# Rotary embedding over split heads: the cosine and sine tables loaded in pieces of 120 and 8 partitions

## The chip, the cores and the metric

The kernel runs on one core of one Trainium2 chip. The core has a matrix engine (PE, TensorE), a vector engine (DVE), a scalar engine (ACT), a general engine (POOL, GpSimd), a queue engine (SP, SyncE) and sixteen DMA engines, which all transfers share. The metric is the device time of one execution in microseconds; a comparison takes the median of several executions. The profiles come from one further execution each, taken by the hardware profiler; "span" is the time from its first to its last instruction.

## The reference

The input x has 16 batches, 512 positions and 1024 columns in float32; the columns are 16 heads of 64. Each head is split in two halves of 32, and the halves are rotated by tables that depend on the position alone:

```
x = x.reshape(batch, seq, num_heads, head_dim)
x1, x2 = x[..., :half_dim], x[..., half_dim:]
cos = cos[None, :, None, :]      # tables are (512, 32)
sin = sin[None, :, None, :]
rotated = concatenate([x1 * cos - x2 * sin, x1 * sin + x2 * cos], axis=-1)
```

33.6 MB go in and 33.6 MB come out; each table has 64 KB.

## The kernel before

All memory is laid out by hand, and each engine has its own list of instructions; the order of work is set by these lists and by semaphores, not by a scheduler.

**Tiles.** The work is ten tiles. Batches 0, 1, 14 and 15 are tiles of their own ("singles"): 128 partitions, 4 positions of 1024 numbers in each (2 MB). The other twelve batches go in six pairs: 128 partitions, 8 positions in each (4 MB). A position row of a tile, 128 x 1024, is one unit of compute; there are 64 units. x lies in a ring of 40 rows, in which the result replaces the input, so the first six tiles find free room and the last four wait for a store to free theirs.

**Compute.** For a unit, DVE multiplies x by cosine into PSUM (L293), POOL multiplies x with its halves swapped by the signed sine into SBUF (L257; six units are done by DVE at L286), and the sum is made in one of two ways: DVE adds (L304), or PE adds the sine product onto the PSUM tile by a matmul with the identity (L224) and ACT copies the sum back (L191).

**Tables.** Cosine and sine are each loaded once into `stage`, as 128 partitions of 4 positions x 32 numbers (L174, 512 bytes in each partition). For singles DVE copies cosine into PSUM (L264), and ACT writes sine with its two signs to SBUF (L182, L183). Pairs hold two batches over 128 partitions, and so need each position in two partitions: PE makes that from `stage` with a picking matrix (L208), ACT writes the signed sine of it (L186, L187). The picking matrix is made by ACT (L177) from an identity that POOL builds (L235, L237).

**Queues.** All loads are issued by ACT (L153 and L174), all stores by SP (L161). ACT's list begins with load 0, then cosine, then sine, then loads 1 to 5, and only then its compute; the last four loads stand between its later additions, each after a wait for the store that frees its room. A transfer adds 16 to its semaphore. Those who use the tables wait for 16 on `sem_cos` (DVE ahead of L264, PE ahead of L208) and on `sem_sin` (ACT ahead of L182, PE ahead of L208). POOL's first product waits for ACT's L183, and SP's first store for the last sum of tile 0.

Of the kernel before, what the change touches and what calls it, by code (L numbers as in the profile page):

```python
# [6 lines left out]
def bass_split_heads_rope_kernel(  # L7
# [20 lines left out]
    P = 128  # L28
    R1 = seq // P
# [34 lines left out]
    EH = H * HD // BANK  # L64
    LEAD = 1
    LAG = 10

    with ExitStack() as stack:
        x_sb = stack.enter_context(nc.sbuf_tensor([P, RING, H, 2, HALF], fp32))
        t2_sb = stack.enter_context(nc.sbuf_tensor([P, NT2, H, 2, HALF], fp32))  # L70
        stage = stack.enter_context(nc.sbuf_tensor([P, 2, R1 * HALF], fp32))
# [11 lines left out]
        sem_cos = stack.enter_context(nc.semaphore("cos"))  # L83
        sem_sin = stack.enter_context(nc.semaphore("sin"))
# [16 lines left out]
        def c_of(t, r):  # L101
            return c1_ps[:, r, :] if tiles[t][1] == R1 else pair_ps[:, r // R1, 0, r % R1, :]
# [19 lines left out]
        def where(u):  # L122
            t, r = rows[u]
            return t, r, u % RING

        def swapped(k):
            return x_sb[:, k, :, ::-1, :]

        def over_heads(table):
            return table[:, None, :, :].broadcast_to([P, H, 2, HALF])  # L130
# [8 lines left out]
        def wait_t2_free(eng, u):  # L139

            if u >= NT2:
                v = u - NT2
                if PE2[v]:
                    eng.wait_ge(sem_e, n_pe[v])
                else:
                    eng.wait_ge(sem_v, n_comb[v])

        def stores_of(k):

            return sum(b * R1 // R2 == k for b, _ in tiles)  # L150

        def load(eng, t):
            eng.dma_start(in_sbuf(t), in_dram(x1, x2, t)).then_inc(sem_in[t], 16)  # L153
# [10 lines left out]
        def on_scalar(ae):  # L164
            later = {}
            for t, (b, n) in enumerate(tiles):
                if b * R1 + n <= RING:
                    load(ae, t)
                else:

                    later.setdefault((b * R1 - RING) // R2 * R2 + R2 - 1 + LAG, []).append(t)
                if t == 0:
                    for i, (table, sem) in enumerate(((cos, sem_cos), (sin, sem_sin))):
                        ae.dma_start(stage[:, i, :], table.rearrange("(s r) d -> s (r d)", r=R1)).then_inc(sem, 16)  # L174

            ae.wait_ge(sem_i, 2)
            ae.activation(  # L177
                pick[:], ident[:].rearrange("q (s k) -> q k s", k=2)[:, :, :, None].broadcast_to([P, 2, P // 2, 2]), COPY
            ).then_inc(sem_g, 1)
            ae.wait_ge(sem_sin, 16)  # L180
            sv = stage[:, 1, :].rearrange("s (r d) -> s r d", d=HALF)
            ae.activation(s1_sb[:, :, 0, :], sv, COPY, scale=-1.0)  # L182
            ae.activation(s1_sb[:, :, 1, :], sv, COPY).then_inc(sem_s, 1)  # L183
            ae.wait_ge(sem_t, 2)
            s2 = s2_sb[:].rearrange("p (k r) t d -> p k r t d", r=R1)
            ae.activation(s2[:, :, :, 0, :], pair_ps[:, :, 1, :, :], COPY, scale=-1.0)  # L186
            ae.activation(s2[:, :, :, 1, :], pair_ps[:, :, 1, :, :], COPY).then_inc(sem_s, 1)  # L187
            for u in range(NU):
                if PE2[u]:
                    ae.wait_ge(sem_e, n_pe[u])  # L190
                    ae.activation(xs[:, u % RING, :], t1_ps[:, u % NT1, :], COPY).then_inc(sem_a, 1)  # L191
                for t in later.get(u, ()):
                    k = (tiles[t][0] * R1 - RING) // R2
                    ae.wait_ge(sem_out[k], 16 * stores_of(k))
                    load(ae, t)

        def on_tensor(pe):
            pe.wait_ge(sem_z, 1)
            for k in range(NT1):
                for b in range(EH):  # L200
                    pe.matmul(  # L201
                        t1_ps[:, k, b * BANK:(b + 1) * BANK], zero[:, 0:P], zero[:], start=True, stop=True
                    ).then_inc(sem_w, 1)
            pe.wait_ge(sem_g, 1)
            pe.wait_ge(sem_cos, 16)
            pe.wait_ge(sem_sin, 16)
            for k in range(2):
                pe.matmul(  # L208
                    pair_ps[:, k].rearrange("p c r d -> p (c r d)"),
                    pick[:, k].rearrange("q s b -> q (s b)"),  # L210
                    stage[:].rearrange("q c f -> q (c f)"),
                    start=True,
                    stop=True,
                ).then_inc(sem_t, 1)
            for u in range(NU):
                if not PE2[u]:
                    continue
                pe.wait_ge(sem_m, u + 1)

                if not V2[u]:  # L220
                    pe.wait_ge(sem_p, n_pool[u])
                t2 = t2_sb[:, u % NT2, :, :, :].rearrange("p h t d -> p (h t d)")
                for b in range(EH):
                    ins = pe.matmul(  # L224
                        t1_ps[:, u % NT1, b * BANK:(b + 1) * BANK],
                        ident[:],
                        t2[:, b * BANK:(b + 1) * BANK],
                        start=False,
                        stop=True,
                        skip_group_check=True,  # L230
                    )
                ins.then_inc(sem_e, 1)
# [27 lines left out]

        def on_vector(ve):
            ve.memset(zero[:], 0.0).then_inc(sem_z, 1)  # L262
            ve.wait_ge(sem_cos, 16)
            ve.tensor_copy(c1_ps, stage[:, 0, :].rearrange("s (r d) -> s r d", d=HALF)).then_inc(sem_c, 1)  # L264
            ve.wait_ge(sem_c, 1)
            ve.wait_ge(sem_w, NT1 * EH)

            def pair_tables():
                ve.wait_ge(sem_s, 2)
                row = pair_ps[:, V_ROW // R1, 1, V_ROW % R1, :]  # L270
                ve.tensor_scalar_mul(v_ps[:, 0, :], row, -1.0).then_inc(sem_c, 1)
                ve.tensor_copy(v_ps[:, 1, :], row).then_inc(sem_c, 1)

            first_v = V2.index(True)

            def mul(u):
                t, r, k = where(u)
                if r == 0:
                    ve.wait_ge(sem_in[t], 16)
                if (t, r) == (2, 0):  # L280
                    pair_tables()
                if u == first_v:
                    ve.wait_ge(sem_c, 3)
                if V2[u]:
                    wait_t2_free(ve, u)
                    ve.tensor_tensor(t2_sb[:, u % NT2, :, :, :], swapped(k), over_heads(v_ps), mult)  # L286
                if u >= NT1:
                    v = u - NT1
                    if PE2[v]:
                        ve.wait_ge(sem_a, n_pe[v])  # L290
                    else:
                        ve.wait_ge(sem_v, n_comb[v])
                ve.tensor_tensor(  # L293
                    t1_ps[:, u % NT1, :].rearrange("p (h d) -> p h d", d=HALF),
                    x_sb[:, k, :, :, :].rearrange("p h t d -> p (h t) d"),
                    c_of(t, r)[:, None, :].broadcast_to([P, 2 * H, HALF]),
                    mult,
                ).then_inc(sem_m, 1)

            def comb(u):  # L300
                t, r, k = where(u)
                ve.wait_ge(sem_m, u + 1)
                ve.wait_ge(sem_p, n_pool[u])  # L303
                ve.tensor_tensor(  # L304
                    xs[:, k, :],
                    t1_ps[:, u % NT1, :],
                    t2_sb[:, u % NT2, :, :, :].rearrange("p h t d -> p (h t d)"),
                    add,
                ).then_inc(sem_v, 1)

            for u in range(NU + LEAD):
                if u < NU:
                    mul(u)
                if u >= LEAD and not PE2[u - LEAD]:
                    comb(u - LEAD)

        on_sync(nc.sync)
        on_scalar(nc.scalar)
        on_gpsimd(nc.gpsimd)
        on_tensor(nc.tensor)  # L320
        on_vector(nc.vector)


# [31 lines left out]
```

## Time and profile before

| what | value |
|---|---|
| time, median of 3 runs | 161.21 us (161.02 to 161.35) |
| span of the profiled execution | 160.3 us |
| moved by DMA | 67.26 MB, 419 GB/s over the span |
| HBM read and written | 33.69 MB and 33.55 MB |
| DVE, POOL busy | 130.3 us, 134.9 us |
| PE, ACT busy | 72.8 us, 24.4 us |
| loads of x, 4 MB: issue to landing | 38.0 us (median of 6) |
| stores, 4 MB: issue to landing | 25.0 us (median of 6) |
| cosine, sine: issue to landing | 7.8 us, 7.5 us |

In lines of the profile, times are in microseconds. In the page's slices each digit is a share of 1/40 of the span, in tenths. A group's line names the source line, the engine, the operation and its tiles. In the timeline the first number is the start, the second the duration, and brackets tell how long the engine stood idle before and what ended that. In the table of stretches a row begins with the stretch and its length, then come the busy times of PE, PE's weight load, DVE, ACT and POOL, the clock granted to PE, the share of time in which the DMA engines were busy, and GB/s. A waits line gives the sum, the number of waits and the longest. "ACTq" and "SPq" are the queues' issuing of transfers.

The trace also records each packet of the DMA engines with its start, duration and size (not the engine it ran on), and each increment that a transfer makes on its semaphore when it lands.

### The profile page before, as it was taken

The numbers are of one execution on the slowest core, as the hardware profiler recorded it, in microseconds if no ns is written. First come the engines' busy times: TensorE is split into PE (matmuls) and PEld (weight loads), VectorE is DVE, ScalarE is ACT, GpSimd is POOL, SyncE is SP. The second block draws the span as 40 slices with busy tenths as digits, with TensorE's granted clock in tenths as the row PEclk, the third lists the DMA queues.
The fourth block names the chain that finished last, engine by engine and source line by source line (L and its number), as shares of the span: only waits on it lengthen the run. The fifth ranks groups of instructions, "written<-read, shape, count | busy, mean of one in ns | idle before, by whom it ended". The sixth has DMA issues, their size and how long they took to land.

```text
span 160.3 us, 522 instructions
## 1 busy us (share of the span) xinstructions
PE 72.8 (45%) x94; PEld 24.0 (15%) x94; DVE 130.3 (81%) x117; ACT 24.4 (15%) x27; POOL 134.9 (84%) x64
## 2 busy tenths in 40 slices
PE   6050004478357936660847105489458435850000
PEld 1020002022202211210221002022202111220000
DVE  0069998599989999996999709899889999999500
ACT  0420000203120222022012010201220402040000
POOL 1059999999999999999999999699999999289400
PEclk9955555557755587689687965555555977699555
DMA  5999999999999999999999999999999999999896
GB/s 147 409 441 474 409 450 409 425 429 429 446 429 458 417 411 466 409 433 401 450 433 425 425 409 458 409 433 433 411 429 462 441 417 401 450 441 441 376 450 294
DMA packets 3170, 67.26 MB, mean 419 GB/s; under 512 B 352, under 2 KB 608, under 8 KB 608
## 3 DMA queue, kind: packets, MB, share of 16 engines
q10 hardware_dynamic: 1728, 33.69, 49.6%
q1 hardware_dynamic: 1440, 33.56, 48.9%
q14 instruction: 2, 0.02, 0.0%
HBM read 33.69 MB, written 33.55 MB: 419 GB/s over the span
## 4 chain that ended last, share of the span: by engine, by line
DMA 60%; POOL 13%; DVE 8%; PE 7%; issue 3%; ACT 2%; ACTq 1%; DVEq 0%
DMA x_sb<-in_x_dram 41%; DMA out_dram<-x_sb 18%; POOL t_sb L257 13%; PE t_ps L224 7%; DVE t_ps L293 5%; DVE x_sb L304 3%; ACT x_sb L191 2%; ACTq L153 1%; ACTq L174 1%; DVE t_sb L286 0%; DVEq L303 0%
## 5 line engine op out<-in xcount | busy, mean ns | idle before, releaser
L257 POOL TENSOR_TENSOR t_sb<-x_sb,s_sb 128x1024 f32<-128x1024 f32 x58 | 134.2, 2346 | 14.8 <-ACT s_sb L183 8.5
L224 PE MATMUL t_ps<-t_sb,ident 128*128 128x512 f32 x84 | 68.0, 957 | 63.0 <-DVE t_ps L293 39.2
L293 DVE TENSOR_TENSOR t_ps<-x_sb,pair_ps 128x1024 f32<-128x1024 f32 x48 | 57.7, 1223 | 9.9 <-ACT x_sb L191 9.8
L304 DVE TENSOR_TENSOR x_sb<-t_ps,t_sb 128x1024 f32<-128x1024 f32 x43 | 52.4, 1218 | 2.6 <-POOL t_sb L257 2.6
L224 PEld LDWEIGHTS t_ps<-t_sb,ident 128*128 128x128 f32 x84 | 22.1, 290 | 108.9 <-DVE t_ps L293 74.6
L191 ACT ACTIVATE x_sb<-t_ps 128x1024 f32<-128x1024 f32 x21 | 21.5, 1023 | 109.9 <-PE t_ps L224 96.9
L293 DVE TENSOR_TENSOR t_ps<-x_sb,tab_ps 128x1024 f32<-128x1024 f32 x16 | 19.3, 1222 | 0.1
L286 DVE TENSOR_TENSOR t_sb<-x_sb,tab_ps 128x1024 f32<-128x1024 f32 x6 | 7.3, 1213 | 0.0
L264 DVE COPY tab_ps<-stage 128x128 f32<-128x128 f32 x1 | 0.3, 294 | 7.8 <-DMA stage<-in_cos_dram 7.8
L208 PE MATMUL pair_ps<-stage,pick 128*128 128x256 f32 x4 | 2.0, 667 | 5.4 <-DMA stage<-in_sin_dram 5.4
L201 PE MATMUL t_ps<-zero 128*128 128x512 bf16 x6 | 2.7, 627 | 1.3 <-DVE zero L262 1.3
L208 PEld LDWEIGHTS pair_ps<-stage,pick 128*128 128x128 f32 x4 | 1.2, 324 | 6.4 <-issue 6.3
L177 ACT ACT_TABLE_LOAD x1 | 1.3, 1283 | 5.5 <-issue 5.5
L201 PEld LDWEIGHTS t_ps<-zero 128*128 128x128 bf16 x6 | 0.7, 136 | 2.4 <-DVE zero L262 1.2
L262 DVE MEMSET zero<- 128x256 uint32 x1 | 0.3, 272 | 0.9 <-PEq L337 0.9
L186 ACT ACTIVATE s_sb<-pair_ps 128x256 f32<-128x256 f32 x1 | 0.4, 383 | 1.7 <-PE pair_ps L208 1.7
L182 ACT ACTIVATE s_sb<-stage 128x128 f32<-128x128 f32 x1 | 0.3, 309 | 2.1 <-DMA stage<-in_sin_dram 2.1
L235 POOL MEMSET ident<- 128x128 f32 x1 | 0.2, 204 | 0.3 <-POOLq L337 0.3
L177 ACT ACTIVATE pick<-ident 128x256 f32<-128x256 f32 x1 | 0.4, 416 | 0.0
L187 ACT ACTIVATE s_sb<-pair_ps 128x256 f32<-128x256 f32 x1 | 0.4, 379 | 0.0
L237 POOL TENSOR_SCALAR_AFFINE_SELECT ident<-ident 128x128 f32<-128x128 f32 x1 | 0.3, 292 | 0.1
L337 POOL MEMSET const-float32-0.0<- 128x1 f32 x1 | 0.1, 98 | 0.3 <-issue 0.3
(6 smaller groups left out, 1.0 us busy)
## 6 DMA issues: line engine op xcount, KB each, us to landing
x_sb<-in_x_dram ACTq DMA_DIRECT2D x6, 4096.0 KB, 38.0
out_dram<-x_sb SPq DMA_DIRECT2D x6, 4096.0 KB, 25.0
x_sb<-in_x_dram ACTq DMA_DIRECT2D x4, 2048.0 KB, 22.6
out_dram<-x_sb SPq DMA_DIRECT2D x4, 2048.0 KB, 15.2
stage<-in_cos_dram ACTq DMA_DIRECT2D x1, 64.0 KB, 7.8
stage<-in_sin_dram ACTq DMA_DIRECT2D x1, 64.0 KB, 7.5
```

Source lines behind the costliest of these rows:

```text
L153: eng.dma_start(in_sbuf(t), in_dram(x1, x2, t)).then_inc(sem_in[t], 16)
L174: ae.dma_start(stage[:, i, :], table.rearrange("(s r) d -> s (r d)", r=R1)).then_inc(sem, 16)
L177: ae.activation(pick[:], ident[:].rearrange("q (s k) -> q k s", k=2)[:, :, :, None].broadcast_to([P, 2, P // 2, 2]), COPY).then_inc(sem_g, 1)
L186: ae.activation(s2[:, :, :, 0, :], pair_ps[:, :, 1, :, :], COPY, scale=-1.0)
L191: ae.activation(xs[:, u % RING, :], t1_ps[:, u % NT1, :], COPY).then_inc(sem_a, 1)
L201: pe.matmul(t1_ps[:, k, b * BANK:(b + 1) * BANK], zero[:, 0:P], zero[:], start=True, stop=True).then_inc(sem_w, 1)
L208: pe.matmul(pair_ps[:, k].rearrange("p c r d -> p (c r d)"), pick[:, k].rearrange("q s b -> q (s b)"), stage[:].rearrange("q c f -> q (c f)"),
L224: ins = pe.matmul(t1_ps[:, u % NT1, b * BANK:(b + 1) * BANK], ident[:], t2[:, b * BANK:(b + 1) * BANK], start=False, stop=True, skip_group ...
L257: pl.tensor_tensor(t2_sb[:, u % NT2, :, :, :], swapped(k), over_heads(s_of(t, r)), mult).then_inc(sem_p, 1)
L286: ve.tensor_tensor(t2_sb[:, u % NT2, :, :, :], swapped(k), over_heads(v_ps), mult)
L293: ve.tensor_tensor(t1_ps[:, u % NT1, :].rearrange("p (h d) -> p h d", d=HALF), x_sb[:, k, :, :, :].rearrange("p h t d -> p (h t) d"), c_of ...
L304: ve.tensor_tensor(xs[:, k, :], t1_ps[:, u % NT1, :], t2_sb[:, u % NT2, :, :, :].rearrange("p h t d -> p (h t d)"), add,).then_inc(sem_v, 1)
```

## The change

Each table is loaded by two transfers in place of one: partitions 0 to 119 first, then partitions 120 to 127. Both pieces of a table add 16 to the same semaphore, and all who wait for a table wait for 32. The order on ACT's queue is load 0, cosine's 120 partitions, cosine's 8, sine's 120, sine's 8, load 1 and so on. No compute instruction is changed. In the changed kernel all lines behind the edit stand 2 to 4 lines further down.

```
+    MOST = 15 * 8
...
                 if t == 0:
                     for i, (table, sem) in enumerate(((cos, sem_cos), (sin, sem_sin))):
-                        ae.dma_start(stage[:, i, :], table.rearrange("(s r) d -> s (r d)", r=R1)).then_inc(sem, 16)
+                        rows_of = table.rearrange("(s r) d -> s (r d)", r=R1)
+                        for part in (slice(0, MOST), slice(MOST, P)):
+                            ae.dma_start(stage[part, i, :], rows_of[part]).then_inc(sem, 16)
...
-            ae.wait_ge(sem_sin, 16)
+            ae.wait_ge(sem_sin, 32)
             sv = stage[:, 1, :].rearrange("s (r d) -> s r d", d=HALF)
...
             pe.wait_ge(sem_g, 1)
-            pe.wait_ge(sem_cos, 16)
-            pe.wait_ge(sem_sin, 16)
+            pe.wait_ge(sem_cos, 32)
+            pe.wait_ge(sem_sin, 32)
...
             ve.memset(zero[:], 0.0).then_inc(sem_z, 1)
-            ve.wait_ge(sem_cos, 16)
+            ve.wait_ge(sem_cos, 32)
```

## The prediction

> **What bounds the kernel now.** I read the page from its second part downwards, because a change to two small transfers can matter only through the DMA engines or through whoever waits for the tables.
>
> ```profile
> span 160.3 us, 522 instructions
> ...
> PE 72.8 (45%) x94; PEld 24.0 (15%) x94; DVE 130.3 (81%) x117; ACT 24.4 (15%) x27; POOL 134.9 (84%) x64
> ...
> DMA  5999999999999999999999999999999999999896
> ...
> DMA packets 3170, 67.26 MB, mean 419 GB/s; under 512 B 352, under 2 KB 608, under 8 KB 608
> ...
> q10 hardware_dynamic: 1728, 33.69, 49.6%
> q1 hardware_dynamic: 1440, 33.56, 48.9%
> ```
>
> No compute engine is full: POOL has 84%, DVE 81%. The row of DMA digits is 9 from the second slice almost to the end, and the two queues together took 98.5% of the time of sixteen engines. The table of stretches gives the rate at which a full engine runs:
>
> ```profile
> 4.00:7.00 3.00, 0.00 (x0) 0.00 (x0) 0.00 (x0) 1.52 (x2) 0.00 (x0) 1.00 1.00 426
> 12.00:20.00 8.00, 0.00 (x0) 0.00 (x0) 7.70 (x7) 0.11 (x1) 8.00 (x5) 0.50 1.01 434
> 20.00:150.00 130.00, 68.02 (x84) 22.08 (x84) 118.46 (x106) 21.49 (x21) 123.71 (x54) 0.67 1.00 430
> 150.00:158.00 8.00, 0.00 (x0) 0.00 (x0) 1.23 (x1) 0.00 (x0) 0.30 (x1) 0.50 1.01 434
> ```
>
> The last two columns are the DMA share and GB/s: 1.00 and 426 to 434 everywhere, with loads alone (4 to 20), loads and stores (20 to 150) and stores alone (150 to 158). So an engine moves 27 GB/s (430 divided by 16) and has no free time. In the packets' records the first one starts at 1.82 us and the rest follow back to back. The end is therefore set by how much work the busiest of the sixteen engines has, and compute matters only if it is late enough to leave them empty. How late that is stands in the chain of waits and among POOL's waits:
>
> ```profile
> 93.45 47.51 DMA x_sb<-in_x_dram
> 140.96 0.07 issue
> 141.02 9.29 POOL t_sb L257 x4
> ...
> 150.40 1.23 DVE x_sb L304
> ```
>
> ```profile
> POOL t_sb L257 <- DMA x_sb<-in_x_dram: 4.3, 2, 3.9
> ```
>
> POOL stands idle for 3.9 us before the last load has landed at 140.96. Then 9.3 us of POOL and 1.2 of DVE, and the last store, issued at 151.70, lands at 160.3. That takes 8.6 us, while 2.10 MB at 430 GB/s are 4.9: it stood 3.7 us behind earlier stores. Compute that started up to about 3.7 us later would still meet a full DMA queue.
>
> **The change part by part.** Durations are those of the profiled execution, whose span is 160.3; the median of the runs is 161.21, so 0.9 us lie around the span, and I add what I find to 161.21.
>
> *Two more issues on the ACT queue.* The timeline of ACT has them:
>
> ```profile
> 0.81 0.37 ACTq L153 DMA_DIRECT2D x_sb<-in_x_dram  x1
> 1.21 0.46 ACTq L174 DMA_DIRECT2D stage<-in_cos_dram  x1
> 1.69 0.45 ACTq L174 DMA_DIRECT2D stage<-in_sin_dram  x1
> 2.17 3.27 ACTq L153 DMA_DIRECT2D x_sb<-in_x_dram  x5
> 5.47 1.28 ACT L177 ACT_TABLE_LOAD   x1 [5.47 <-issue]
> 6.76 0.42 ACT L177 ACTIVATE pick<-ident 128x256 f32<-128x256 f32 x1
> 9.26 0.31 ACT L182 ACTIVATE s_sb<-stage 128x128 f32<-128x128 f32 x1 [2.08 <-DMA stage<-in_sin_dram]
> ```
>
> From one table issue to the next is 0.48 us (1.21, 1.69, 2.17), so two more push all behind them by 0.96: the second load of x from 2.17 to 3.13, the function-table load to 6.43, the end of pick from 7.18 to 8.14. Load 0 is issued ahead of them and keeps the engines busy; in the packets' records no engine reaches the tables before 7.5 us, so the second load (issue over at 3.8 instead of 2.83) is still 3.7 us early. The pick is wanted by the matmul of L208, which waits for sine until 9.34: 1.2 us of cover left of 2.2. Other issues on this queue took 0.33 to 2.02 us. At 2.02 each the shift would be 4.0: the second load would be issued around 6.2 to 6.9, still ahead of 7.5, while pick would end at 11.2, sine's copies and so POOL would start 2 us late, inside POOL's 3.9. Cost: 0, from 0 to about 0 even at the far end. The SP queue (stores) and POOL's are not touched.
>
> *What a table costs a DMA engine.* Take the stretch 7.4 to 8.8 us, in which the tables pass:
>
> ```profile
> DMA packets 331, 0.57 MB, mean 410 GB/s; under 512 B 48, under 2 KB 304, under 8 KB 304
> ...
> q10 hardware_dynamic: 331, 0.57, 106.4%
> ```
>
> Of 331 packets 256 are table rows (2 x 128 rows of 512 B) and 48 are the closing ones (three transfers, sixteen each; the whole run has 352 for 22 transfers, 16 each). The other 27 are 16 KB pieces of x, each 16384 B / 27 GB/s = 0.61 us. Engine time is 1.064 x 16 x 1.4 = 23.8 us; less 27 x 0.61 = 16.5 leaves 7.3 for 304 small packets: 24 ns each. Today each engine has 2 x 8 rows and 2 closing packets of tables, 18 x 24 = 0.43 us.
>
> *Closing packets.* Two more transfers close on at least one and at most sixteen engines each: 2 to 32 more packets, on one engine at most two, 0.05 us.
>
> *Who carries the rows.* The bytes stay the same, only the shares can move. How 120 and 8 rows are dealt to sixteen engines no row of this trace shows, for all its transfers have 128 or 64 rows. Gain side: an engine gets no table at all and is 0.43 us lighter; that is worth something only if it ends last, and only as far as the next one. The sixteen increments that each transfer leaves in the trace give that margin: the last store's come from 159.11 to 160.30, the last but one at 160.27, so 0.03 us. For the first load the last came at 8.77 and the one before at 8.52: 0.25. Loss side: one engine gets all eight rows of both small pieces, 16 more rows and 2 closing packets, +0.43, if that engine ends last. In between, eight rows on eight engines: two rows and two closing packets more on each, 4 x 24 = +0.10 at most. The nearest row is today's transfer, which is dealt evenly (sixteen closing packets for 128 rows), so I take an even deal of each piece: -0.03 to +0.10, middle +0.03.
>
> The Trainium skill (DMA: Bandwidth & Descriptors, section "Why a DMA increments its semaphore by 16 and not by 1") says that a transfer runs on the largest number of engines up to 16 that divides its outermost dimension, and on the lowest-numbered ones; that would be 15 and 8 engines here, no table on the sixteenth. By it eight engines get +0.10 or less, seven nothing and one -0.43; no run so far shows it.
>
> *Waits.* Line 174's semaphores now count to 32, so DVE's copy (L264), ACT's L182 and the matmul of L208 wait for both pieces. In the trace, DVE's copy starts at 9.04 and ACT's at 9.26, 0.22 us apart for two transfers; another two of the same kind behind one another, with half the rows each on average, can't add more than 0.44. Behind them stand the first multiply of DVE (9.37) and of POOL (9.85), and behind these the first store (20.48). A shift of 0.44 lies within the 3.7 worked out above. If that cover were gone it would cost its full 0.44. It stays: 0.
>
> A rule speaks against the change: the same page's "Anatomy of one DMA" gives each DMA about 2.0 us of fixed cost, and its "Rules for kernel authors" calls two transfers to disjoint partitions not worth doing. Serial payment for two more would make 165.2. The trace disagrees as to serial payment, since cosine and sine landed 0.22 us apart.
>
> *Sum.* Issues 0, waits 0, engine shares +0.03: 161.21 + 0.03 = 161.2 us.
>
> **The rivals.** About 0.2% (0.32 us) is what a measurement of this kernel can tell from no change.
>
> Faster: the relieved engine is the one that ends last, by more than this execution shows. For it: one engine is last by 0.25 us in the first load, 0.22 in the second (14.05 after 13.83) and in the third (23.76 after 23.54), which looks like one late engine. Against it: from 37 us on it no longer stands alone, and at the end the margin is 0.03. With the early margin the time is 161.21 - 0.25 = 160.96; with the whole relief 160.78. To pass 0.2% it needs 0.32 of 0.43.
>
> Slower: the eight rows of each table go through one engine. Place: the small pieces, right behind load 0. Price: 0.43 us on that engine for the whole run, for it never has a pause to catch up; 161.64. It decides from 0.32/0.024 = 13 more small packets on one engine, so from six more rows per table, and only if that engine is among those that end last. Against it is the even deal of today. The far end of this, all 120 rows on one engine, is 240 x 24 ns = 5.8, less today's 0.4: 166.6; I give it 3%.
>
> Hidden anyway with another mix: the same bytes, but loads and stores meet at other moments. The rate varied from 426 to 434 between full stretches; half a percent in a tenth of the run is 0.08 us, and runs of one kernel already span 161.02 to 161.35. This spreads the forecast by some 0.2 us both ways.
>
> That the change does nothing of what it says is out: the instruction list has a 120x128 and an 8x128 transfer per table in place of one of 128x128.
>
> **How the numbers follow.** No change to be told: 0.46. Faster: 0.22 for the relieved engine and 0.05 for another mix, 0.27. Slower: 0.16 for the piled rows, 0.03 for their far end, 0.08 for another mix, 0.27. The time is that of the forecast, 161.2. The range runs from the whole relief (160.78) to the piled rows (161.64 plus the two closing packets' 0.05): 160.8 to 161.7.
>
> **What would show it.** In the changed profile: the DMA share again 1.00 at 426 to 434 GB/s from 12 to 158 us, rows of 512 B again 256, closing packets 352 plus 2 to 32 (their number tells the engines used; 14 more by the rule of the skill); the second load issued near 3.1; DVE's copy between 8.7 and 9.5; POOL's idle time before the last load still above 3 us. The faster rival would show as the last store's latest increments lying closer to the others, the slower one as a single late increment, 0.3 us or more behind the next, in every landing from the tables on. I am wrong in the mechanism if the DMA share drops after 12 us, or if an engine has gaps while the second load is awaited.

## The result and the profile after

| | median, us | runs | ratio to before (95%) |
|---|---|---|---|
| before | 161.38 (161.02 to 161.94) | 6 | |
| changed | 164.09 (163.83 to 166.42) | 6 | 1.0163 (1.0146 to 1.0180) |

The change makes the kernel 2.6 us slower by the ratio (2.7 by the medians). Executions of one kernel can differ by several microseconds (of 68 of the kernel before in all these comparisons, five took 164.6 to 166.6 us), and a ratio leaves out those that lie over 1.5% above the fastest. Where a span and the time of the same execution are both known, 1.4 us lie around the span (162.8 and 164.25 here; 159.9 and 161.34 for the kernel before), not the 0.9 that I took: the profiled execution of before was longer than the median.

The page of the changed kernel:

```profile
span 162.8 us, 524 instructions
...
DMA  5999999999999999999999999999999999999893
...
DMA packets 3184, 67.26 MB, mean 413 GB/s; under 512 B 366, under 2 KB 622, under 8 KB 622
```

The same bytes, and 366 closing packets in place of 352: 14 more, as 15 and 8 engines for each table give. The digits look like those of before; only the last one is lower. The table of stretches (DMA share and GB/s are the last two columns) shows where the time is:

```profile
4.00:7.00 3.00, 0.00 (x0) 0.00 (x0) 0.00 (x0) 0.89 (x1) 0.00 (x0) 1.00 1.00 426
12.00:20.00 8.00, 0.00 (x0) 0.00 (x0) 7.32 (x7) 0.49 (x2) 8.00 (x5) 1.00 1.04 449
20.00:140.00 120.00, 64.02 (x80) 20.32 (x80) 109.54 (x99) 19.46 (x19) 115.08 (x50) 0.70 1.01 429
140.00:150.00 10.00, 3.47 (x5) 1.20 (x4) 7.60 (x8) 2.05 (x2) 6.53 (x3) 0.67 0.97 419
150.00:158.00 8.00, 0.00 (x0) 0.00 (x0) 2.99 (x3) 0.00 (x0) 2.74 (x2) 0.50 0.91 389
```

The kernel before has, for the longest of these stretches:

```profile
20.00:140.00 120.00, 65.66 (x80) 21.20 (x80) 109.13 (x98) 19.44 (x19) 114.73 (x50) 0.66 1.01 430
```

Up to 140 us nothing is lost to the eye (429 GB/s, and 430 before). From 150 to 158 the DMA engines were full before (1.01, 434 GB/s), and now some of them have nothing to do (0.91, 389). The chain of waits names what they lack:

```profile
94.09 49.31 DMA x_sb<-in_x_dram
143.40 0.07 issue
143.47 9.28 POOL t_sb L261 x4
```

The last load lands at 143.40 in place of 140.96, 2.4 us later; the spans differ by 2.5. After it everything goes as before: 9.3 us of POOL, then the last store. POOL waits 6.1 us for that load (3.9 before):

```profile
POOL t_sb L261 <- DMA x_sb<-in_x_dram: 7.1, 2, 6.1
```

The increments of that load, one for each engine, tell how it is late. Before, eight engines end at 138.49 to 139.48 and eight at 140.59 to 140.96. Now twelve end at 138.58 to 140.51 and four at 142.89 to 143.40. So four engines are late, and the other twelve are not.

Where this begins can be seen in the DMA queues just when the first store comes in. Queue q1 carries stores, q10 loads. First the kernel before, from 23.6 to 24.9 us, then the changed one, from 24.1 to 24.9:

```profile
q10 hardware_dynamic: 15, 0.49, 91.5%
q1 hardware_dynamic: 8, 0.13, 23.5%
```

```profile
q10 hardware_dynamic: 9, 0.29, 85.8%
q1 hardware_dynamic: 4, 0.07, 19.1%
```

The first numbers are packets. In the packets' records each engine starts its first store packet where one of its load packets ends (a load packet of 32 KB takes 1.21 us). Before the change eight engines started their first store packet in the first round (23.90 to 24.46 in the packets' records) and the other eight after one more load packet (24.98 to 25.21). With the change it is four (24.31 to 24.70) and twelve (25.16 to 25.66). The next load to land shows the same numbers: its increments come within 0.52 us on twelve engines and 0.96 to 1.34 us after the first of them on four. At the last load these four increments are 4.31 to 4.82 us after the first. So here the engines that take the store early are late with their loads from there on, and the lag grows. (The records don't name the engine; that the four are the same ones rests on their number.)

The start, on ACT and its queue, went as worked out:

```profile
1.21 1.01 ACTq L178 DMA_DIRECT2D stage<-in_cos_dram  x2
2.25 0.87 ACTq L178 DMA_DIRECT2D stage<-in_sin_dram  x2
3.15 2.93 ACTq L155 DMA_DIRECT2D x_sb<-in_x_dram  x5
...
9.64 0.31 ACT L186 ACTIVATE s_sb<-stage 128x128 f32<-128x128 f32 x1 [1.81 <-DMA stage<-in_sin_dram]
```

The second load is issued at 3.15, and nothing waits for it. Sine's last piece lands 0.63 us after load 0 (9.61 and 8.98) where it took 0.47 (9.24 and 8.77), and load 0 itself lands 0.21 later. That is no accident of one execution: load 0 lands at 8.91 to 9.25 in all five profiled kernels of this document that load the tables in pieces, and at 8.57 to 8.77 in ten of the eleven others; why was not found. POOL starts at 10.23 in place of 9.85, and the first store is issued at 20.86 in place of 20.48, first before and then changed:

```profile
20.48 0.38 SPq L161 DMA_DIRECT2D out_dram<-x_sb  x1
```

```profile
20.86 0.37 SPq L163 DMA_DIRECT2D out_dram<-x_sb  x1
```

### The profile page after: what moved, and what is told of

It is laid out like the page before. It is cut to its first block, busy times and chain, and to the rows that moved or that the text cites. A ratio compares the mean times of both kernels' runs of the same rounds, so it can differ in the third digit from the quotient of the medians.

```text
span 162.8 us, 524 instructions
## 1 busy us (share of the span) xinstructions
PE 72.3 (44%) x94; PEld 23.4 (14%) x94; DVE 130.4 (80%) x117; ACT 24.4 (15%) x27; POOL 134.8 (83%) x64
## 4 chain that ended last, share of the span: by engine, by line
DMA 60%; POOL 27%; issue 3%; DVE 2%; ACTq 2%; DVEq 0%; SPq 0%
DMA x_sb<-in_x_dram 41%; POOL t_sb L261 27%; DMA out_dram<-x_sb 18%; DVE x_sb L308 1%; ACTq L178 1%; DVE t_ps L297 1%; ACTq L155 1%; DVEq L307 0%; SPq L139 0%
## 5 line engine op out<-in xcount | busy, mean ns | idle before, releaser
L228 PEld LDWEIGHTS t_ps<-t_sb,ident 128*128 128x128 f32 x84 | 21.5, 283 | 109.7 <-DVE t_ps L297 64.8
L297 DVE TENSOR_TENSOR t_ps<-x_sb,tab_ps 128x1024 f32<-128x1024 f32 x16 | 19.3, 1222 | 2.7 <-DMA x_sb<-in_x_dram 2.3
```

The costliest lines, as they stand in the source:

```text
L228: ins = pe.matmul(t1_ps[:, u % NT1, b * BANK:(b + 1) * BANK], ident[:], t2[:, b * BANK:(b + 1) * BANK], start=False, stop=True, skip_group ...
L297: ve.tensor_tensor(t1_ps[:, u % NT1, :].rearrange("p (h d) -> p h d", d=HALF), x_sb[:, k, :, :, :].rearrange("p h t d -> p (h t) d"), c_of ...
```

## The experiments

Four theories were set against each other. U: the uneven deal of the rows over the engines. I: the two further transfers themselves, by issue or by wait. L: a later start of compute. P, which became S: the moment at which the first store meets the load packets. In every diff the lines that reserve room or a semaphore are left out, and code between the shown lines is marked by dots or left out. Medians are over all runs; "before" was run beside each set, with medians of 161.34 to 161.54.

**Two even halves** (e1_halves). Edit of the changed kernel:

```
-    MOST = 15 * 8
+    MOST = 64
```

> Each table in two pieces of 64 and 64 partitions: as many issues, waits and late starts as the change, but each piece is dealt to all sixteen engines alike. Theory U (the uneven deal of 120 and 8 rows sets four engines out of step, and they lose 2.5 us later): as before, 161.0 to 161.9 us, the last store's sixteen increments within 1.5 us. Theory I (the two further transfers themselves, by issue or by wait): 163.8 to 164.3. Theory P (any small shift of the start changes which engines lose time): anything between 160 and 166, not like either.

Measured: 164.49 us (163.42 to 165.12), ratio 1.0188 (1.0143 to 1.0233). The page counts 384 closing packets, so each of the four pieces ran on all sixteen engines, and the loss is still there. Theory U falls. First store at 20.94, four engines first, last load at 144.00.

**Compute later, transfers untouched** (e2_late_start). Edit of the kernel before, on ACT:

```
             sv = stage[:, 1, :].rearrange("s (r d) -> s r d", d=HALF)
+            for i in range(2):
+                ae.activation(spare[:, i], sv, COPY)
             ae.activation(s1_sb[:, :, 0, :], sv, COPY, scale=-1.0)
```

> The kernel before, its tables in one transfer each, with two idle copies of sine on ACT ahead of the signed ones, so that POOL and with it the first store start some 0.4 us later, as they did after the change (10.23 in place of 9.85 us). Theory L (stores that start 0.4 us later meet the loads at other moments): near 164. Theories U and I: as before, 161.0 to 161.9. Theory P: anything.

Measured: 161.91, 166.14, 167.16 and 168.84 us. No transfer was changed, and in three of four executions a loss is there, larger than that of the change; a ratio can't be given. In the profiled execution, the slowest of them, POOL starts at 10.13, the first store is issued at 20.75, one engine takes it ahead of the others (and two a packet behind them), and the last load lands at 148.00. Theory I does not explain this run; L and P are left.

**Two further transfers for which no compute waits** (e3_dummy120, e4_dummy8; only SP waits for them, behind the last store). Edit of the kernel before, with 0:120 in the one and 120:128 in the other:

```
                         ae.dma_start(stage[:, i, :], table.rearrange("(s r) d -> s (r d)", r=R1)).then_inc(sem, 16)
+                    for i in range(2):
+                        ae.dma_start(spare[0:120, i, :], sin.rearrange("(s r) d -> s (r d)", r=R1)[0:120]).then_inc(sem_x, 16)
```

> The kernel before, with two further loads of 120 rows of 512 bytes into unused room behind sine, for which nobody waits. Fifteen engines get 16 rows more than the sixteenth, as in the change; tables, waits and compute are those of before. Theory U, if the light engine is what counts: 163.5 to 164.8. Theory I by waits, and L: as before plus at most 0.4 us of rows, 161.2 to 162.2. Theory P: anything.

> The kernel before, with two further loads of 8 rows of 512 bytes into unused room behind sine, for which nobody waits: eight engines get two rows and two closing packets more than the other eight, as in the change, but no engine is relieved. Theory U, if the eight heavier engines are what counts: 163.5 to 164.3; if the light one is: 161.0 to 162.0. Theory I by issue: near 164; by wait: as before. Theory P: anything.

Measured: 161.87 us (ratio 1.0032, 1.0019 to 1.0045) and 161.29 us (1.0009, 0.9990 to 1.0028). The same number of issues ahead of load 1, and engines as unequal as in the change (sixteen rows in the one, two in the other), cost only the rows: 0.5 us for 18 small packets on fifteen engines, and nothing to be told for the others (though one of e4's ten executions took 165.25). With e2 this leaves what the waits do: they move the start of compute. In e4 sine had landed early (9.07), the first store was issued at 20.30, and all sixteen engines took it in one round.

**The same delay, longer** (e5_change_late3, e6_before_late4, e7_before_late6, e8_before_late8). The edit of e2 with more copies: three in the changed kernel, four, six and eight in the kernel before.

> The changed kernel with three idle copies of sine on ACT ahead of the signed ones, which puts the first store, and all compute, a further 0.6 us later. Theory S (the first store must reach all sixteen DMA engines within one round of their 1.21 us load packets; a minority that takes it a round earlier than the rest is slowed for the rest of the run): the arrival moves from 0.3 us ahead of the last engine's slot into the gap behind it, all sixteen take the first store in one round, and the time falls to 161.0 to 161.8 although everything starts later. Theory L (a later start costs by being later): 164 or more. Theory I (the further transfers or waits cost in themselves): 164.

> The kernel before with four idle copies, so the first store is 0.8 us later. Theory S: the arrival moves from 0.5 us ahead of the last engine's slot to 0.3 behind it, into the gap; all sixteen engines in one round in place of eight and eight; 160.8 to 161.5, last store's increments within 1 us. Theory L: later than the run with two copies, so 166 or more.

> The kernel before with six idle copies, first store 1.23 us later: one whole load packet. Theory S: as before, eight engines and eight, 161.0 to 161.9. Theory L: 166 or more.

> The kernel before with eight idle copies, first store 1.64 us later: one load packet more than the run with two copies. Theory S: as that run, one to four engines apart from the rest, 162 to 169 and scattered. Theory L: above all the others.

Measured: 163.22 us (1.0099, 1.0073 to 1.0125), 162.35 (1.0070, 1.0042 to 1.0097), 162.29 (1.0051, 1.0034 to 1.0068) and 162.09 (1.0027, 1.0008 to 1.0047). Theory L falls: with two to four times the copies of e2 compute starts later than there (POOL at 10.51 to 11.57 in e6 to e8, 10.13 in e2) and costs a fraction of it. But S's own numbers failed too. I had taken the store to reach all engines at one moment, so that the split could be read from the load packets and would come back after one packet's time. The engines ahead were 10, 13, 4 and 13 where I expected 16, 16, 8 and 1 to 4. What held is that there is a bad stretch, and that later than it the loss is smaller.

**Sine first** (e9_change_sine_first, e10_before_sine_first). Edit of both kernels:

```
-                    for i, (table, sem) in enumerate(((cos, sem_cos), (sin, sem_sin))):
+                    for i, (table, sem) in ((1, (sin, sem_sin)), (0, (cos, sem_cos))):
```

> The changed kernel with sine's two pieces ahead of cosine's, so that the same four transfers and the same waits stand, but sine lands, and POOL and the first store start, some 0.3 us earlier, about where they were before the change (store issued near 20.5 us in place of 20.86). Theory S (what counts is when the first store meets the load packets; bad is 20.7 to 20.95 us): 161.0 to 162.2. Theory I (the four transfers or their waits cost in themselves): 163.8 to 164.5.

> The kernel before with sine ahead of cosine: one transfer each, the first store some 0.2 us earlier, near 20.3, where the run with two 8-row loads had it. Theory S: 160.8 to 161.6. If any shift of the first store costs: above 162.

Measured, e9: ten executions, 161.29, 161.57, 161.68, 161.69, 162.29, 163.40, 163.75, 165.17, 166.42 and 166.90 us; ratio 1.0032 (0.9998 to 1.0066). With all four transfers and their waits the kernel can run at the time of before, so they don't cost 2.6 us by themselves; it stands at the edge. The profiled execution was the slowest of them, with the store at 20.68, two engines first, and the last load at 146.05. Measured, e10: 161.34 us (0.9996, 0.9983 to 1.0009), no faster than before. It shows the orderly case, though. From 23.7 to 24.9 us all sixteen engines take the store:

```profile
q10 hardware_dynamic: 14, 0.46, 93.0%
q1 hardware_dynamic: 16, 0.26, 50.9%
```

**The first store alone held back** (e11_store_relay1, e12_store_relay4). Edit of the kernel before, one copy and four:

```
                     wait_added(sp, u)
+                    if t == 0:
+                        sp.wait_ge(sem_x, 1)
...
+            ae.wait_ge(sem_v, n_comb[R1 - 1])
+            for i in range(1):
+                ae.activation(spare[:, i], sv, COPY).then_inc(sem_x, 1)
             for u in range(NU):
                 if PE2[u]:
```

> The kernel before with the first store alone held back: ACT, which is idle then, waits for tile 0's last sum, makes one idle copy, and SP waits for that ahead of the first store (issue 0.3 to 0.5 us later, 20.8 to 21.0). Tables, loads, waits of compute and all other stores stand as before. Theory S: 163 to 168, as the change or as the run with two copies. Theory L (compute that starts later) and theory I: as before, 161.0 to 161.9.

> As the run before, with four idle copies: the first store alone is held back by 0.9 to 1.1 us, to about 21.5. Theory S: past the bad stretch, 161.0 to 162.5. If a later first store costs by its lateness: more than the run with one copy. Theory I: 161.0 to 161.9.

Measured: 167.58 us (165.76 to 168.39), ratio 1.0341 (1.0263 to 1.0420), and 162.47 us (162.37 to 162.88), 1.0067 (1.0046 to 1.0089). This is the plainest of the runs. One store of ten is issued 0.25 us later than in the kernel before, and the kernel is 6 us slower; the same one issued 0.77 later costs 1 us. The timeline of e11 around it:

```profile
20.34 0.31 ACT L194 ACTIVATE spare<-stage 128x128 f32<-128x128 f32 x1 [8.37 <-DVE x_sb L311]
20.73 0.37 SPq L165 DMA_DIRECT2D out_dram<-x_sb  x1
```

The queues of e11 from 23.9 to 24.9 us, where three engines go ahead (nine follow by 25.36, and four more a packet later, from 26.34), and its row for 150 to 158 us, where some engines stand empty (0.71, 303 GB/s) because the last load lands at 146.19:

```profile
q10 hardware_dynamic: 9, 0.29, 70.5%
q1 hardware_dynamic: 3, 0.05, 11.5%
```

```profile
150.00:158.00 8.00, 0.00 (x0) 0.00 (x0) 5.77 (x5) 0.00 (x0) 5.52 (x3) 0.50 0.71 303
```

**The same in the changed kernel, and a control** (e13_change_relay4, e14_sine_first_relay1). The edit of e12 in the changed kernel, and that of e11 in e10.

> The changed kernel with the first store alone held back by four idle copies on ACT (0.8 us later than 20.86); tables, waits, compute and all else as in the change. Theory S (a small group of DMA engines that takes the first store a round ahead of the rest loses time for the rest of the run): out of the bad stretch, 161.5 to 163.0, faster than the changed kernel although its store is later. Theory I (the further transfers or their waits): 163.8 to 164.5 or more.

> The kernel before with sine ahead of cosine (first store at 20.14 us) and the first store alone held back by one idle copy on ACT, to about 20.4, where the kernel before has it (20.48). Theory S: half or more of the engines take the first store in the first round, 161.1 to 162.0. If the copy and the wait that hold the store back cost by themselves: 164 or more, as in the run that held back the store of the kernel before.

Measured, e13: 162.79 us (162.66 to 163.41), ratio 1.0104 (1.0079 to 1.0128), below the interval of the change. Its first store is issued at 22.02, 1.2 us later than in the change, everything else is the change, and it is 1.3 us faster. The other 1.4 us stay: e12, the kernel before with the same copies and wait, loses 1.1 too. Measured, e14: 161.98, 166.39, 168.58 and 168.61 us, three of them far from the 161.1 to 162.0 that I expected. The store went out at 20.59, not 20.4, and in the profiled execution four engines took it first. So it can't serve as a control for the copy and the wait. These are bounded by e12, which has the same wait and more copies and lost 1.1 us in all.

All profiled executions together. Each engine's packets follow one another without a break, so they can be joined, end to start, to sixteen chains from 20 to 32 us. "Groups" counts the engines by the start of their first store packet; a new group begins where the next engine is more than 0.45 us later.

| kernel | store issued | groups | last load landed | span |
|---|---|---|---|---|
| e10 | 20.14 | 16 | 140.32 | 159.8 |
| e4 | 20.30 | 16 | 140.43 | 159.8 |
| e3 | 20.48 | 15, 1 | 141.13 | 160.6 |
| before | 20.48 | 8, 8 | 140.96 | 160.3 |
| e6 | 21.14 | 13, 3 | 140.79 | 161.4 |
| e8 | 22.19 | 13, 3 | 140.31 | 160.9 |
| e5 | 21.79 | 10, 6 | 140.30 | 161.1 |
| e12 | 21.25 | 11, 5 | 140.01 | 161.1 |
| e13 | 22.02 | 10, 6 | 140.65 | 161.3 |
| e7 | 21.51 | 4, 12 | 140.16 | 160.8 |
| after | 20.86 | 4, 12 | 143.40 | 162.8 |
| e1 | 20.94 | 4, 12 | 144.00 | 163.4 |
| e14 | 20.59 | 4, 12 | 145.52 | 165.0 |
| e11 | 20.73 | 3, 9, 4 | 146.19 | 165.6 |
| e9 | 20.68 | 1, 1, 14 | 146.05 | 165.5 |
| e2 | 20.75 | 1, 13, 2 | 148.00 | 167.4 |

Every profiled execution with a last load later than 142 has a small group of one to four engines ahead at the first store, and every store issued between 20.59 and 20.94 gave one. In these six the increments of the last load show the number again: four, four, four, three, two and one of them (after, e1, e14, e11, e9, e2) come over 2 us behind the others. e7 is the exception: four ahead, with a full 0.98 us between the groups (0.46 in the changed kernel), and no late load; its four come 1.1 to 2.0 us behind the others, which come early there (up to 138.13).

## Why the prediction was wrong

The prediction named a sign of a wrong mechanism: a DMA share that drops after 12 us. It came, with 0.91 from 150 to 158 us.

**Issues on the ACT queue: right.** The second load was issued at 3.15 (3.13 worked out) and pick ended at 7.83, ahead of sine. e3 and e4 have two issues more at the same place and no loss beyond their rows.

**What a table costs an engine: right.** 24 ns a packet gave 0.43 us for 18; e3 puts 18 more on fifteen engines and is 0.5 us slower.

**Who carries the rows: right that it is worth nothing to be told,** by e1 against the change and by e4. 14 further closing packets agree with the Trainium skill's rule (DMA: Bandwidth & Descriptors, "Why a DMA increments its semaphore by 16 and not by 1"): 15 and 8 engines. Each table's semaphore also shows two increments at issue (1.99 and 2.38 us for cosine) and 23 at landing, as that section says of a transfer that uses fewer than sixteen engines.

**Waits: the step that failed.** I put a shift of 0.44 us or less on the first store and wrote that it "lies within the 3.7 worked out above", cost 0. The shift was 0.38 in the profiled executions, 0.16 of it between load 0 and sine and 0.21 from the later load 0, which the prediction did not have. The 3.7 us of cover hold for compute as such: e6 to e8 start it 0.7 to 1.7 us later and lose 1.1 to 0.4, the latest the least. But the first store is not only late work that a full queue hides. It is where a second queue joins sixteen engines that are already full, and the time of joining decides which engines take a store before their next load. e11 moved nothing but that, by 0.25 us, and lost 6 us.

**"Hidden anyway with another mix": the right place, sized wrongly.** I had the rival that loads and stores meet at other moments, and priced it from the rates of full stretches (426 to 434 GB/s) at 0.08 to 0.2 us. Those rates are means over sixteen engines. The price is set by the slowest one: the last load waits for every engine, so four engines that are 2.4 us behind cost 2.4 us while the mean rate from 20 to 140 us is 429 GB/s against 430. The prediction reads the increments of the first three loads and of the last store, but not those of the last load, where the kernel before already shows two groups of eight, 1.1 us apart.

**The rule against the change.** The skill's "Rules for kernel authors" advises against two transfers to disjoint partition halves, and the change and e1 are slower, by 1.6% and 1.9%. The 2 us for each transfer of "Anatomy of one DMA" are not what it costs: that section gives them for transfers issued from GpSimd, these are issued by ACT, and two more of them cost nothing that can be told in e4. Nor did either rival of the prediction decide it: no engine was relieved to any gain (faster), and no rows piled on one (slower).

**What stays open.** In step, packets keep their time: in e10, from 25 to 140 us, the 16 and 32 KB packets that take over 50 ns more than their usual time (0.61 and 1.21 us) lose 1.1 us over all engines. In the kernel before it is 12.0, in the change 18.9, in e11 31.4. So packets are longer where the engines are out of step. This sum alone does not set the loss, for e12 has 19.3 and no late load. What parts the six executions with a late load from the ten others is where it lies: 9 to 19 us of it in packets of stores, against 6.5 or less. That the engines slow each other, by which resource, and why a small group's lag in loads grows more in some executions than in others (e7), was not shown; the records don't name the engine of a packet. Nor is the moment at which a store reaches each engine known well enough to compute the split beforehand, as e5 to e8 and e14 showed.

## What to carry to other kernels

Where loads and stores run on two queues over DMA engines that are already full, look at the increments of single engines, above all those of the last load, and not at mean rates: a group that lags sets the end. A shift of some tenths of a microsecond in the first transfer of the second queue can then be worth several per cent, so a small change upstream of it is judged only with that moment held fixed, or moved by itself in a run of its own. Two kernels here have all sixteen engines in step (e4 and e10) and are no faster than the median of the kernel before.

## What was not expected of the hardware

One store of 2 MB issued 0.25 us later made a kernel of 161.4 us take 167.6 (e11), and another one took from 161.29 to 166.90 us in ten executions (e9). With the engines in step the spread of the last store's sixteen increments was 0.74 and 0.92 us (e4, e10); in the kernel before it was 1.20, in the changed one 2.52.
